# Instruction order from the timeline simulation in place of the default scheduler

## The chip, the cores and the metric

One core of one Trainium2 chip runs the whole program. The metric is device time in microseconds (us) of one execution, as the median of several runs. Matmuls run on TensorE (PE, its weight loads shown apart as PEld), elementwise work on VectorE (DVE) and ScalarE (ACT), a little on GpSimd (POOL), and SyncE (SP) issues nearly all DMAs.

## The reference, cut to what matters

Two layers of a hybrid trunk are computed for 128 context tokens and 256 latent tokens of width 1024. All weights are shared, so the kernel treats the tokens as one matrix of 384 columns; the two kinds differ in their modulation, in attention and in the sequence length of the convolutions.

```python
def trunk_layer(x, cond, l, P, cache):
    mod = (jax.nn.silu(cond) @ P['w_mod'][l] + P['b_mod'][l])[:, None, :]
    sh1, sc1, g1, sh2, sc2, g2, sh3, sc3, g3 = jnp.split(mod, N_MOD, axis=-1)
    h = rmsnorm(x, P['g_ffn1'][l]) * (1 + sc1) + sh1
    x = x + 0.5 * g1 * swiglu(h, P['w1_gate'][l], P['w1_up'][l], P['w1_down'][l])
    h = rmsnorm(x, P['g_mix'][l]) * (1 + sc2) + sh2
    m, kv = token_mix(h, l, P, cache)
    x = x + g2 * m
    h = rmsnorm(x, P['g_ffn2'][l]) * (1 + sc3) + sh3
    x = x + 0.5 * g3 * swiglu(h, P['w2_gate'][l], P['w2_up'][l], P['w2_down'][l])
    return x, kv
```

`token_mix` projects h to 2048 columns and splits them into attention (8 query heads, 2 key heads, window and cached context), a conformer convolution of 31 taps with layernorm, and a Hyena mixer (two gated long convolutions, done here by transforms). The three parts are joined by one output projection. The feed-forward width is 2816. Everything is float32.

## The kernel before, in words

Activations stay on chip feature-major: 8 tiles of 128 features by 384 tokens. Every large product is made of 128x128 weight blocks. Each float32 operand is split into a rounded high part and the low rest, and `mm3` (L262 to L265) issues three matmuls for one block: high by high, high by low, low by high. The weights come as one stream of 313 chunks of 8 blocks (512 KB each) in the order in which the program is traced. `blk` (L241) loads a chunk into one of 5 `raw` buffers, ScalarE rounds it to `hi` (L249), VectorE subtracts to get `lo` (L250); there are 4 `hi` and 4 `lo` buffers, so weights can stand ready up to four chunks ahead. One chunk feeds 24 matmuls.

The modulation vectors need 128 more loads of 512 KB (`mod_unit`, L317). They share the 5 `raw` buffers with the stream, and VectorE makes two multiply-accumulate passes (L324) over each. These units are spread over the feed-forward stages by a table (`MODS`).

The stages follow each other: a start (`startup`: modulation of the first sublayer, the Hyena filters, the first four column tiles of the first product, and dummy matmuls from `spin`, L1055), feed-forward 1 of layer 0, mix of layer 0, feed-forward 2, and the same for layer 1, ending with `last_down`. In a feed-forward stage the order of the matmuls is fixed by data: gate and up tile by tile into two PSUM buffers each (`acc`, `S`), then the down projection. In a mix stage, generators for Hyena (`hyena`, `spectral`: transposes L695, transforms L674, products on VectorE L706 to L712, inverse transforms L720), the conformer (L764, L362, L382), attention scores (L843, softmax on VectorE and ScalarE, transposes L900), values (L910) and the output projection are traced between the 16 tiles of the input projection, by the list `PROGRAM`.

What sets the order on the chip: each engine runs its own instructions strictly in the order in which the program lists them, and waits on semaphores for data and buffers of the others. That list isn't the traced order. The framework traces the kernel, gives each instruction a priority by its place in the trace (`high_priority` moves it ahead: 94 places for loading and splitting a chunk, 100 for loading a modulation unit, 400 for the second half of a pair), and then plays the program on a simulated core. Whenever an engine of that core can take work, it is handed the instruction of the best priority among those whose inputs and buffers are there. The order in which work was handed out becomes the order of the lists; buffers are given out in the same pass. So the order depends on how long the simulated core takes over each step. `keep_in_program_order` pins the dummy matmuls behind what was traced before them on TensorE, and `after` pins pairs of small matmuls together.

## Time and profile before

| what | value |
|---|---|
| time, median of 3 runs (lowest, highest) | 1510.45 us (1509.03, 1514.73) |
| the profiled execution: time, span of its instructions | 1510.81 us, 1509.0 us |
| TensorE busy, weight loads busy | 98%, 93% of the span |
| VectorE, ScalarE busy | 74%, 45% |
| mean granted TensorE clock | 0.993 |
| DMA moved | 260.97 MB, mean 173 GB/s |

The profile covers one execution. Busy time is the union of an engine's instruction spans; a matmul's span overlaps the next one's, so a busy TensorE may still run under its pace. The clock is the share of full speed that was granted.

### The profile page before, as it was taken

The numbers are of one execution on the slowest core, as the hardware profiler recorded it, in microseconds if no ns is written. First come the engines' busy times: TensorE is split into PE (matmuls) and PEld (weight loads), VectorE is DVE, ScalarE is ACT, GpSimd is POOL, SyncE is SP. The second block draws the span as 40 slices with busy tenths as digits, with TensorE's granted clock in tenths as the row PEclk, the third lists the DMA queues.
The fourth block names the chain that finished last, engine by engine and source line by source line (L and its number), as shares of the span: only waits on it lengthen the run. The fifth ranks groups of instructions, "written<-read, shape, count | busy, mean of one in ns | idle before, by whom it ended". The sixth has DMA issues, their size and how long they took to land.

```text
span 1509.0 us, 22131 instructions
## 1 busy us (share of the span) xinstructions
PE 1482.5 (98%) x8372; PEld 1401.0 (93%) x8372; DVE 1116.2 (74%) x2115; ACT 673.3 (45%) x1164; POOL 29.7 (2%) x72
## 2 busy tenths in 40 slices
PE   8999999999999999999999999999999999999997
PEld 4799999999968999999999999999996799999885
DVE  6799998776896789897558998755599577555342
ACT  6673333335476653224336333333547665333331
POOL 0100000000000000000000000000000000000000
PEclk9899999999999999999999999999999999999999
DMA  9847876565312357676444777644431135444531
GB/s 312 301 151 249 270 261 227 189 204 181 118 64 70 112 189 237 219 235 209 154 135 133 247 244 237 225 154 155 143 125 49 59 109 167 154 154 140 182 112 42
DMA packets 72651, 260.97 MB, mean 173 GB/s; under 512 B 8224, under 2 KB 9760, under 8 KB 72544
## 3 DMA queue, kind: packets, MB, share of 16 engines
q1 hardware_dynamic: 71360, 254.30, 51.4%
q0 software_dynamic: 1184, 5.25, 0.9%
q8 instruction: 66, 1.08, 0.3%
q14 instruction: 41, 0.34, 0.1%
HBM read 252.96 MB, written 6.56 MB: 172 GB/s over the span
## 4 chain that ended last, share of the span: by engine, by line
PE 92%; DVE 3%; ACT 3%; DMA 1%; issue 1%; SPq 0%; POOL 0%; POOLq 0%; DVEq 0%; ACTq 0%
PE acc L263 14%; PE acc L264 14%; PE acc L265 14%; PE S L265 12%; PE S L263 12%; PE S L264 12%; PE sp L474 2%; PE at L474 2%; PE sp L674 2%; PE acc L474 1%; PE S L474 1%; PE sp L720 1%; DVE lo L250 1%; DMA raw<-wmod 1%; DMA raw<-wms 0%
## 5 line engine op out<-in xcount | busy, mean ns | idle before, releaser
L250 DVE TENSOR_TENSOR lo<-raw,hi 128x1024 fp32r<-128x1024 f32 x313 | 381.7, 1222 | 209.1 <-ACT hi L249 160.2
L249 ACT CAST hi<-raw 128x1024 fp32r<-128x1024 f32 x313 | 327.0, 1049 | 390.7 <-issue 131.3
L324 DVE SCALAR_TENSOR_TENSOR junk<-raw,cb 128x1024 f32<-128x1024 f32 x256 | 312.7, 1221 | 49.8 <-DMA raw<-wmod 46.8
L263 PE MATMUL acc<-h,hi 128*128 128x384 f32 (+1 forms) x960 | 331.0, 345 | 0.0
L265 PE MATMUL acc<-h,lo 128*128 128x384 f32 (+1 forms) x960 | 326.0, 340 | 0.5 <-DVE lo L250 0.5
L264 PE MATMUL acc<-h,hi 128*128 128x384 f32 (+1 forms) x960 | 325.4, 340 | 0.6 <-DVE h L918 0.6
L263 PE MATMUL S<-h,hi 128*128 128x384 f32 (+1 forms) x768 | 259.9, 338 | 1.0 <-DVE x L435 1.0
L265 PE MATMUL S<-h,lo 128*128 128x384 f32 (+1 forms) x768 | 259.5, 338 | 0.0
L264 PE MATMUL S<-h,hi 128*128 128x384 f32 (+1 forms) x768 | 259.4, 338 | 0.0
L264 PEld LDWEIGHTS acc<-h,hi 128*128 128x128 f32 x960 | 181.0, 189 | 5.8 <-issue 3.1
L263 PEld LDWEIGHTS acc<-h,hi 128*128 128x128 f32 x960 | 180.5, 188 | 6.1 <-issue 3.9
L265 PEld LDWEIGHTS acc<-h,lo 128*128 128x128 f32 x960 | 181.5, 189 | 2.0 <-issue 0.8
L263 PEld LDWEIGHTS S<-h,hi 128*128 128x128 f32 x768 | 144.5, 188 | 2.0 <-issue 1.9
L265 PEld LDWEIGHTS S<-h,lo 128*128 128x128 f32 x768 | 145.0, 189 | 0.4 <-issue 0.3
L264 PEld LDWEIGHTS S<-h,hi 128*128 128x128 f32 x768 | 144.6, 188 | 0.4 <-issue 0.4
L393 ACT ACTIVATE h<-x,mod 128x128 fp32r<-128x128 f32 x96 | 41.5, 453 | 91.3 <-DVE x L435 89.4
L531 DVE TENSOR_TENSOR t<-S,t 128x384 f32<-128x384 f32 x72 | 39.8, 552 | 20.5 <-PE S L265 20.5
L281 ACT CAST P<-t 128x384 fp32r<-128x384 f32 x24 | 12.3, 514 | 71.4 <-DVE t L531 71.4
L530 ACT ACTIVATE t<-acc 128x384 f32<-128x384 f32 x72 | 34.8, 483 | 11.2 <-PE acc L265 11.2
L394 DVE SCALAR_TENSOR_TENSOR h<-x,mod,h 128x128 fp32r<-128x128 f32 x96 | 38.3, 415 | 1.2
L414 DVE TENSOR_TENSOR t<-acc,rb 128x384 f32<-128x384 f32 x44 | 24.3, 552 | 16.3 <-PE acc L265 16.3
L408 ACT ACTIVATE t<-t,mod,mod 128x128 f32<-128x128 f32 x64 | 31.7, 541 | 6.4 <-DVE t L405 6.4
(492 smaller groups left out, 2196.6 us busy)
## 6 DMA issues: line engine op xcount, KB each, us to landing
raw<-stream SPq DMA_DIRECT2D x313, 512.0 KB, 4.0
raw<-wmod SPq DMA_DIRECT2D x128, 512.0 KB, 4.3
raw<-wms SPq DMA_DIRECT2D x16, 512.0 KB, 6.6
Hd<-sw POOLq DMA_DIRECT2D x6, 768.0 KB, 4.6
H<-Hd SPq DMA_DIRECT2D x6, 768.0 KB, 4.9
x<-x SPq DMA_DIRECT2D x8, 192.0 KB, 6.2
y<-h SPq DMA_DIRECT2D x6, 256.0 KB, 2.1
cb<-crow SPq DMA_DIRECT2D x2, 512.0 KB, 5.3
```

Of the source, the lines that this page charges most:

```text
L249: nc.scalar.copy(out=hi, in_=raw)
L250: nc.vector.tensor_tensor(out=lo, in0=raw, in1=hi.bitcast(F32), op=ALU.subtract)
L263: nc.tensor.matmul(out, lhsT=w[0], rhs=x[0], start=start, stop=False)
L264: nc.tensor.matmul(out, lhsT=w[0], rhs=x[1], start=False, stop=False)
L265: nc.tensor.matmul(out, lhsT=w[1], rhs=x[0], start=False, stop=stop)
L324: nc.vector.scalar_tensor_tensor(out=self.junk, in0=raw, scalar=1.0, in1=self.cb[:, ci, :], op0=ALU.mult, op1=ALU.mult, accum_out=m[:, 2 * ...
L393: nc.scalar.mul(out=hl[:, 0, a:b], in_=self.x[k][:, a:b], mul=sc)
L394: nc.vector.scalar_tensor_tensor(out=hl[:, 1, a:b], in0=self.x[k][:, a:b], scalar=sc, in1=hl[:, 0, a:b].bitcast(F32), op0=ALU.mult, op1=AL ...
L408: nc.scalar.activation(out=t[:, a:b], in_=t[:, a:b], func=AF.Identity, scale=A[:, i:i + 1], bias=B[:, i:i + 1])
L474: nc.tensor.matmul(accs[b], lhsT=hid[2 * c + e][xi][:, b * 128:(b + 1) * 128], rhs=w[e][wi], start=c == 0 and left[b] == 5, stop=c == NFF ...
L530: nc.scalar.activation(out=s, in_=gp[:, :T], func=AF.Silu)
L531: nc.vector.tensor_tensor(out=s, in0=up[:, :T], in1=s, op=ALU.mult)
```

## The change

The context in which the kernel is traced gets one more argument. It selects the machine that the scheduler plays the program on: the framework's timeline simulation instead of the simulated core that it uses by default. The traced program, its priorities, its buffers, its pins and every instruction's work are the same; the handing out of work follows the other machine's times, and so the order of the instructions in each engine's list, the places of the DMA issues in SP's list, and which buffer each tile gets may be others.

```diff
--- before.py
+++ after.py
@@ -1197,7 +1197,7 @@
     outs = {"y": (3, 128, D), "nk": (DEPTH, 128, NP), "nv": (DEPTH, 128, NP)}
     for n, s in outs.items():
         d[n] = nc.dram_tensor(n, s, F32, kind="ExternalOutput").ap()
-    with tile.TileContext(nc) as tc, ExitStack() as ctx:
+    with tile.TileContext(nc, schedule_with_timeline_sim=True) as tc, ExitStack() as ctx:
         k = Kernel(ctx, tc, d)
         k.run()
     arrays["stream"] = pack_stream(k.plan, i)
```

## Rows read from the trace of the kernel before

**Rows 1.** The page's first part: engine, busy us, share of span, instructions.
```profile
PE 1482.5 (98%) x8372; PEld 1401.0 (93%) x8372; DVE 1116.2 (74%) x2115; ACT 673.3 (45%) x1164; POOL 29.7 (2%) x72
```
**Rows 2.** Busy time by stage, from the start to the last evacuation (header first).
```profile
core 0: us, PE busy (x) PEld busy (x) DVE busy (x) ACT busy (x) POOL busy (x), PEclk, DMA share, GB/s
0.00:73.00 73.00, 65.75 (x372) 43.17 (x373) 50.33 (x154) 46.88 (x83) 6.11 (x12) 0.91 0.87 306
73.00:346.00 273.00, 272.66 (x1549) 269.34 (x1547) 242.76 (x415) 110.14 (x166) 4.78 (x5) 1.00 0.68 223
346.00:507.00 161.00, 157.71 (x921) 140.25 (x922) 124.03 (x315) 95.01 (x214) 5.39 (x23) 1.00 0.32 104
507.00:780.00 273.00, 273.00 (x1562) 272.44 (x1561) 212.76 (x354) 109.37 (x163) 1.77 (x1) 1.00 0.60 193
780.00:1059.00 279.00, 279.00 (x1598) 278.47 (x1597) 217.41 (x363) 108.83 (x164) 1.45 (x2) 1.00 0.61 195
1059.00:1224.00 165.00, 159.30 (x926) 140.49 (x925) 124.30 (x312) 95.81 (x214) 4.33 (x23) 1.00 0.29 95
1224.00:1499.00 275.00, 275.00 (x1454) 256.88 (x1453) 140.35 (x202) 103.88 (x155) 3.65 (x4) 1.00 0.40 132
1499.00:1509.00 10.00, 0.09 (x1) 0.00 (x0) 4.23 (x8) 3.39 (x7) 2.19 (x3) 0.63 0.41 157
```
**Rows 3.** TensorE's waits, whole run: us in total, times, longest; first and last.
```profile
PE at L293 <- DMA raw<-wms: 2.3, 2, 1.7
PE acc L910 <- ACT pt L903: 2.1, 3, 1.3
...
PE at L900 <- ACT pt L903: 0.5, 2, 0.2
```
**Rows 4.** TensorE's timeline in layer 1's mix: start us, length us, what.
```profile
1130.97 0.42 PE L263 MATMUL acc<-h,hi 128*128 128x386 f32 x1
1131.23 0.34 PE L264 MATMUL acc<-h,hi 128*128 128x386 f32 x1
1131.41 1.94 PE L720 MATMUL sp<-csts,sw 128*128 128x128 f32 x16
1133.11 0.42 PE L265 MATMUL acc<-h,lo 128*128 128x386 f32 x1
1133.37 0.34 PE L263 MATMUL acc<-h,hi 128*128 128x386 f32 x1
```
**Rows 5.** Busy time in shorter stretches, columns as in rows 2.
```profile
60.00:70.00 10.00, 10.00 (x23) 5.09 (x19) 7.08 (x14) 5.14 (x9) 1.00 (x2) 0.56 0.71 252
150.00:200.00 50.00, 50.00 (x286) 50.00 (x285) 49.65 (x79) 17.94 (x24) 0.00 (x0) 1.00 0.83 272
600.00:650.00 50.00, 50.00 (x289) 50.00 (x287) 41.98 (x63) 16.75 (x24) 0.00 (x0) 1.00 0.69 220
1140.00:1150.00 10.00, 8.57 (x45) 5.27 (x45) 9.19 (x26) 6.17 (x21) 0.00 (x0) 1.00 0.14 52
1160.00:1170.00 10.00, 8.79 (x54) 5.39 (x53) 9.70 (x33) 8.63 (x23) 0.00 (x0) 1.00 0.16 54
```
**Rows 6.** Costliest groups on VectorE and ScalarE: busy us, mean ns, idle before.
```profile
L250 DVE TENSOR_TENSOR lo<-raw,hi 128x1024 fp32r<-128x1024 f32 x313 | 381.7, 1222 | 209.1 <-ACT hi L249 160.2
L249 ACT CAST hi<-raw 128x1024 fp32r<-128x1024 f32 x313 | 327.0, 1049 | 390.7 <-issue 131.3
L324 DVE SCALAR_TENSOR_TENSOR junk<-raw,cb 128x1024 f32<-128x1024 f32 x256 | 312.7, 1221 | 49.8 <-DMA raw<-wmod 46.8
```
**Rows 7.** The page's DMA issues: count, KB each, us from issue to landing.
```profile
raw<-stream SPq DMA_DIRECT2D x313, 512.0 KB, 4.0
raw<-wmod SPq DMA_DIRECT2D x128, 512.0 KB, 4.3
```

## The prediction

> **What bounds the kernel now.** I read the page's busy shares first, then the same busy times cut by stage, then TensorE's waits, and last the timeline of a mix stage. The shares say that TensorE is the bound: busy 1482.5 of 1509.0 us, VectorE behind it with 74% [rows 1]. The reader should see in the stages that this isn't one regime. The four feed-forward stages (273, 273, 279 and 275 us, together 1100 us) have TensorE busy throughout, but for 0.34 us in the first [rows 2]. There 289 matmuls start in 50 us, one per 0.173 us [rows 5]; a chunk of 24 lasts 4.2 us. The rest is the start (73 us, 7.3 us idle), the two mixes (161 us with 3.3 idle, 165 us with 5.7 idle) and a tail of 10 us in which TensorE has one matmul and VectorE, ScalarE and the output DMAs finish [rows 2]. TensorE's waits are short: fifteen rows between 2.3 and 0.5 us in total, the longest single one 1.7 us, for a DMA of the start; the second row is a chain of the mix, TensorE waiting for ScalarE's copy ahead of the values [rows 3]. So no stage but the start, the mixes and the tail can get shorter by order, and every stage can get longer.
>
> In the mixes the engine that decides is VectorE: 9.19 and 9.70 of 10 us busy in two stretches of layer 1's mix, where TensorE is down to 8.57 and 8.79 [rows 5]. The chains (Hyena, conformer, attention) go through VectorE at each step, and what is ahead of a chain's step in its list delays the chain.
>
> **The change part by part.** Nothing is removed or added: the same 8372 matmuls and the same 2115 VectorE instructions [rows 1] in another order. Its price is only what waits come or go, stage by stage. Not known from the trace is how the other machine spaces its steps. What the trace does show is how the order before treats a chain. In layer 1's mix the sixteen inverse-transform matmuls stand between the second and the third matmul of one block [rows 4]: the chain's step was put in front of filler at the first moment it was ready, and the filler, 0.173 us each, gave way. A machine that takes work into a queue ahead of a busy engine fixes the order earlier: filler that is ready gets in first, and the chain's step stands behind it although its priority is better. I take it that the timeline simulation does so to some degree. It is an assumption about the scheduler; the last rival drops it.
>
> Mixes. In a mix the Hyena chain passes between TensorE and VectorE at six steps (transposes, transforms, inverse transforms, twice). No row shows such a step standing behind filler. From below: a gain of all of the mixes' idle time, 3.3 + 5.7 = 9.0 us [rows 2]. From above: one whole chunk of filler, 4.2 us, at each of six steps in both mixes, 12 x 4.2 = 50 us. In between stands the longest piece of VectorE's filler, one `lo` of 1.222 us [rows 6]; with VectorE at 92 to 97% there [rows 5], an early chosen `lo` would lie in the way at each step. I take that, 12 x 1.222 = 14.7 us, because it is the nearest row in size to the waits that chains make now (longest 1.3 us, rows 3). The cover for the rest is TensorE's own filler, of which the projection's tiles provide 16; it is used up about when TensorE's waits begin, near 1140 us, and after that each delay of the chain shows in full.
>
> Start. In 60 to 70 us the granted clock was 0.56, a mean of its two levels (1.2 and 2.4 GHz), and 23 matmuls ran [rows 5]; at full clock the same stretch would have been (1 - 0.56) x 10 = 4.4 us shorter. Another order can spare this or make a second one: from -4.4 - 2.3 (the waits for the first DMAs, rows 3) = -6.7 to, say, two more, +8.8 us. The filters' and modulation's chains share VectorE as the mixes' do, so I take half of one more: +2.2 us.
>
> Here a rule bears on the mixes. The granted clock stays at 1.00 there in spite of TensorE's idle 1.2 to 1.4 us per 10 [rows 5], so lost time is priced at its own length. The Trainium skill (TensorE: Matmul & The Clock Gate, What's actually happening) says that half rate is the default state and activity releases it, so longer idling would also slow the matmuls that follow. By the row a wait costs itself; by the rule the new order's waits, were they much longer than these, would cost up to one stretch like that at 60 us per mix more, 2 x 4.4 us by that row, and the sum would be 1536 us. The start agrees with the rule, the mixes don't reach it, and I leave it out of the sum.
>
> Feed-forward. The weights stand up to four chunks ahead; with one in use that is 3 x 4.2 = 12.6 us of cover. A `lo` put behind one modulation unit is 2 x 1.221 us late [rows 6], and behind two units 4.9 us, which the cover hides, and so it hides a late load of 4.0 us [rows 7]. Below: there is 0.34 us to gain. I take 0. What it costs without the cover is the second rival. The tail: its chain is a fixed sequence for three blocks of 128 tokens, 0.
>
> Sum: 14.7 + 2.2 = 16.9 us, on the profiled execution's 1510.81 us (span 1509.0 and 1.8 around it) 1527.7; that execution lies 0.4 us above the median of the runs, which gives 1527 us. Own range: 1516 (a third of the sum) to 1557, where attention's twelve units per mix are each a `lo` late as well (24 x 1.222 = 29.3 us more).
>
> **The rivals.** *The loads bunch up and the feed-forward starves.* Stream and modulation share five raw buffers, and VectorE is busy 49.65 of 50 us at 150 to 200 us [rows 5], so lost cover isn't rebuilt at once. Were five modulation units loaded in a row, VectorE would owe 5 x 2.44 = 12.2 us before the next chunk's buffer is free; then come the load (4.0 us, rows 7), `hi` (1.05) and `lo` (1.22, rows 6): 18.5 us against a cover of 12.6, a stall of 5.9 us. The 128 units make at most 25 such bunches; a third of them, 8 x 5.9 = 47 us, gives 1557, and with the forecast's terms 1574. For it: the DMA issues are reordered too. Against it: the units are traced a few per tile, and the stream's loads have nearly the same lead in priority.
>
> *Faster: the chains are placed better.* If the timeline simulation's times are nearer to the chip's than the default's, the order has fewer steps that come to an engine before their input. It decides from the point where the chains' waits on TensorE shrink instead of grow. Price: all of the mixes' idle time, 9.0 us, and about half of the start's 7.3 us idle (its DMAs move 306 GB/s, rows 2, and set part of it), together 12.6 us: 1498. Against it: VectorE is nearly full in those stretches, and no order makes its work less. The weight loads show more room than the busy time: idle 161 - 140.25 and 165 - 140.49, together 45 us in the mixes [rows 2]. The Trainium skill (Perfetto Trace Analysis, Identifying the Most-Contended Engine) says to judge TensorE's headroom by the weight loads' share and not by matmul busy time; by that the limit here would be 45 us and the time down to 1465. The trace agrees only in part: by the matmul rows 9.0 of the 45 us are idle, and how much of the rest is gap no row tells.
>
> *No change.* The order comes out the same where it matters, or the moves lie under the covers named above: the priorities, pins and buffers are the same, and the feed-forward (73% of the span) is held by data. Then 1510 us, at most some 5 us to either side.
>
> **How the numbers follow.** Forecast 0.38, starved feed-forward 0.14, faster 0.26, no change 0.22. About 0.5% (7.6 us) is what a measurement of this kernel tells from no change, so faster is below 1502.9 and slower above 1518.0. The forecast gives 0.36 to slower and 0.02 to the same (its low end lies under 1518), the starved case 0.14 to slower, the faster case 0.22 to faster and 0.04 to the same, no change 0.22 to the same: 0.22, 0.28, 0.50. The range reaches from 1495, somewhat below the faster case, to 1576, the starved case with the forecast's terms.
>
> **What would show it.** Right: the feed-forward stages keep 273 to 279 us and 289 matmuls per 50 us; the mixes grow by about 7 us each; TensorE's timeline there shows chain steps only between whole runs of filler, no longer inside a block; the longest waits are on VectorE's and ScalarE's chain steps. A stretch of low clock in the start tells that term. A wait for `lo` in a feed-forward stage, behind L324 on VectorE, is the starved case. Mixes under 160 us with idle time near zero are the faster case, and identical lists the last. The prediction is wrong if the change in time comes from the feed-forward or the tail, or if the mixes get shorter.

## The result and the profile after

| | median us (lowest to highest, runs) |
|---|---|
| changed kernel | 1546.43 (1544.86 to 1548.21, 4) |
| kernel before, beside it | 1511.12 (1509.03 to 1514.73, 4) |

The ratio is 1.0231, with a 95% interval of 1.0215 to 1.0246: the new order costs 35 us. The forecast was 1527, +16.5 us on its own base, so the direction was right, and the forecast size was less than half of what came. The profiled execution took 1548.21 us (span 1546.3, mean granted clock 0.976); the one of before had 1510.81 (1509.0, 0.993).

First the page of the changed kernel: its first part, the group of the `lo` on VectorE, and the DMA issues of the stream.

```profile
PE 1494.9 (97%) x8372; PEld 1416.1 (92%) x8372; DVE 1111.1 (72%) x2115; ACT 684.7 (44%) x1168; POOL 28.3 (2%) x72
...
L250 DVE TENSOR_TENSOR lo<-raw,hi 128x1024 fp32r<-128x1024 f32 x313 | 382.2, 1223 | 194.0 <-ACT hi L249 147.9
...
raw<-stream SPq DMA_DIRECT2D x313, 512.0 KB, 4.2
```

The same 8372 matmuls and 2115 VectorE instructions as in [rows 1], with 1223 ns for a `lo` (1222 in [rows 6]) and 4.2 us for a landing (4.0 in [rows 7]): none of these operations got dearer. Two numbers of TensorE moved. TensorE's idle time (span less busy) went from 26.5 to 51.4 us, +24.9, and its busy time from 1482.5 to 1494.9, +12.4 for the same matmuls. Together that is the whole 37.3 us of span.

Next the changed kernel by stage (columns as in [rows 2], the cuts at its own stage ends), then shorter stretches of the start, of two feed-forwards and of the two mixes.

```profile
0.00:92.00 92.00, 73.73 (x378) 49.31 (x378) 54.26 (x160) 54.49 (x89) 6.02 (x12) 0.78 0.76 263
92.00:363.00 271.00, 271.00 (x1535) 269.43 (x1535) 238.19 (x409) 107.53 (x164) 4.11 (x5) 0.99 0.68 221
363.00:533.00 170.00, 158.18 (x915) 141.92 (x914) 122.25 (x307) 95.73 (x214) 4.51 (x23) 0.97 0.29 92
533.00:810.00 277.00, 275.68 (x1577) 275.10 (x1577) 212.86 (x361) 112.50 (x165) 0.85 (x1) 1.00 0.59 192
810.00:1089.00 279.00, 279.00 (x1597) 278.73 (x1596) 215.45 (x363) 111.06 (x164) 2.30 (x2) 1.00 0.61 195
1089.00:1257.00 168.00, 158.68 (x910) 141.08 (x909) 121.03 (x305) 94.97 (x211) 5.54 (x23) 0.96 0.28 94
1257.00:1536.00 279.00, 278.21 (x1471) 260.55 (x1469) 142.56 (x209) 104.99 (x160) 2.69 (x3) 1.00 0.41 131
1536.00:1546.00 10.00, 0.39 (x2) 0.00 (x0) 4.53 (x9) 3.39 (x7) 2.29 (x3) 0.66 0.41 157
...
10.00:20.00 10.00, 3.69 (x18) 0.78 (x17) 2.35 (x6) 7.41 (x10) 0.00 (x0) 0.50 1.03 398
20.00:30.00 10.00, 8.97 (x60) 5.19 (x62) 4.47 (x17) 5.77 (x11) 0.00 (x0) 0.65 0.99 331
30.00:40.00 10.00, 5.27 (x22) 2.05 (x19) 8.03 (x30) 8.98 (x14) 0.00 (x0) 0.69 1.01 328
...
150.00:200.00 50.00, 50.00 (x286) 49.24 (x286) 48.77 (x80) 18.64 (x27) 1.06 (x2) 1.00 0.83 278
650.00:700.00 50.00, 50.00 (x288) 50.00 (x287) 46.64 (x72) 18.05 (x24) 0.00 (x0) 1.00 0.75 246
...
433.10:443.10 10.00, 6.72 (x38) 5.50 (x36) 8.71 (x22) 5.65 (x15) 0.00 (x0) 1.00 0.26 75
443.10:453.10 10.00, 7.45 (x39) 5.47 (x39) 7.91 (x26) 5.23 (x20) 0.00 (x0) 0.66 0.33 112
...
1158.80:1168.80 10.00, 6.75 (x37) 5.40 (x35) 8.48 (x23) 6.07 (x18) 0.00 (x0) 0.91 0.26 88
1168.80:1178.80 10.00, 9.16 (x39) 6.05 (x40) 7.77 (x23) 6.98 (x24) 0.00 (x0) 0.57 0.22 79
```

For the sums below the stages are cut at two marks that exist in every run: the first instruction of line 414 (the first four column tiles of the first feed-forward are finished, which ends the start) and the last residual (line 435) of each stage.

| stage, us | before | after | difference | of it TensorE idle |
|---|---|---|---|---|
| start, to the first L414 | 70.3 | 91.3 | +21.0 | +11.0 |
| rest of layer 0's first feed-forward | 275.8 | 271.9 | -3.9 | -0.4 |
| layer 0: mix, second feed-forward | 160.9, 273.3 | 169.7, 277.6 | +13.0 | +9.9 |
| layer 1: first feed-forward | 278.4 | 278.4 | 0 | 0 |
| layer 1: mix, second feed-forward and tail | 165.6, 284.7 | 168.0, 289.5 | +7.2 | +4.4 |

The reader should see that the feed-forwards run as before (286 and 288 matmuls in 50 us, clock 1.00). Where a second feed-forward is longer, it has got matmuls from the mix: 1580 instead of 1564 in layer 0, and at 0.173 us these 16 are 2.8 of its 4.2 us. The two places that lost time are the start and the mixes, and in both the stretches of low clock stand beside or behind stretches in which TensorE is idle.

TensorE's waits of the changed kernel (us in total, times, longest) answer to [rows 3]:

```profile
PE S L843 <- ACT P L865: 9.7, 4, 3.0
PE sp L720 <- DVE ut L709: 4.3, 2, 2.2
PE sp L954 <- ACT t L938: 4.1, 1, 4.1
PE at L300 <- ACT t L297: 3.4, 2, 3.1
```

Before, no single wait was longer than 1.7 us. Now the three longest are all for ScalarE: in the start 4.1 us for the filter's first sine (L938) and 3.1 for the copy of a modulation (L297), in the mixes 3.0 for the exponentials of the attention (L865).

**The start.** ScalarE's timeline of the changed kernel, to its first modulation copy (start us, length us, what, idle before):

```profile
5.09 1.28 ACT L975 ACT_TABLE_LOAD   x1
12.50 0.63 ACT L975 ACTIVATE pt<-pt 128x512 f32<-128x512 f32 x1 [6.12 <-DMA pt<-ld]
...
13.79 0.61 ACT L975 ACTIVATE pt<-pt 128x512 f32<-128x512 f32 x1
14.42 1.28 ACT L938 ACT_TABLE_LOAD   x1
15.71 0.52 ACT L938 ACTIVATE t<-t 128x384 f32<-128x384 f32 x1
16.25 1.28 ACT L976 ACT_TABLE_LOAD   x1
17.55 3.17 ACT L976 ACTIVATE P<-pt,csts 128x512 f32<-128x512 f32 x5
20.62 0.35 ACT L297 COPY t<-at 128x256 f32<-128x256 f32 x1
```

and the same two instructions in the kernel before:

```profile
10.51 0.52 ACT L938 ACTIVATE t<-t 128x384 f32<-128x384 f32 x1 [5.46 <-DVE t L936]
...
13.82 0.37 ACT L297 COPY t<-at 128x256 f32<-128x256 f32 x1 [0.85 <-PE at L293]
```

The sine stands behind an exponential whose operand is still on its way from DRAM, and comes 5.2 us later; the copy stands behind five decay exponentials and comes 6.8 us later. SyncE's list changed as well. Sixteen loads bring the weights of the first modulation (`raw<-wms`, L239). In the kernel before the seventh and the eighth of them follow each other; in the changed one, loads that are wanted later stand ahead of the eighth (SP's list from the two traces, cut: place in the list, load, us of the issue and of the landing):

```
before                                 after
17 raw<-wms, the 7th   13.81 20.57     17    x<-x (L1088)         13.15 20.64
18 raw<-wms, the 8th   15.98 21.84     18    raw<-wms, the 7th    14.45 21.95
19 raw<-stream         16.41 23.06     19-24 x<-x (L1088), 6      15.72 25.00
20 raw<-wms, the 9th   21.64 25.24     25    q<-ld (L943)         20.66 25.66
21 raw<-wms, the 10th  22.07 28.70     26    ut<-ld (L943)        21.96 26.39
22 x<-x (L1088)        23.50 29.16     27-28 cb<-crow (L1050), 2  22.46 30.08
...                                    29    csts<-cst (L1047)    23.52 35.30
38 q<-ld (L943)        38.75 48.90     30-31 cv<-cw (L1016), 2    24.03 37.75
...                                    32    raw<-wms, the 8th    25.42 38.80
52 csts<-cst (L1047)   70.58 78.56
```

The loads of x, q, ut, cb, csts and cv on the right are 7 x 192 + 2 x 256 + 2 x 512 + 960 + 2 x 288 = 4416 KB, 4.5 MB, which at 398 GB/s (the stretch from 10 to 20 us) is an estimated 11.4 us of loading. In the trace 16.9 us pass between the landings of the seventh and the eighth modulation load (21.95 and 38.80), where before it was 1.3 (20.57 and 21.84). The sixteenth was issued at 35.6 us before and at 58.7 us after, and the first feed-forward's first columns can't end before the last modulation.

**A mix.** TensorE's timeline of the changed kernel in layer 0's mix, first a place early in it, then the first two waits for the exponentials:

```profile
424.90 0.34 PE L264 MATMUL acc<-h,hi 128*128 128x386 f32 x1
425.08 1.05 PE L720 MATMUL sp<-csts,sw 128*128 128x128 f32 x8
425.89 0.42 PE L265 MATMUL acc<-h,lo 128*128 128x386 f32 x1
...
437.78 0.49 PE L843 MATMUL S<-kv,q 64*128 64x128 f32 x4
438.20 1.13 PE L674 MATMUL sp<-ut,csts 128*128 128x256 f32 x4
442.37 0.49 PE L843 MATMUL S<-kv,q 64*128 64x128 f32 x4 [3.03 <-ACT P L865]
445.41 1.65 PE L843 MATMUL S<-kv,q 64*128 64x384 f32 x4 [2.55 <-ACT P L865]
```

and VectorE's in between, where the scores' maximum (L860) has to become the exponential's bias (L861):

```profile
438.83 0.48 DVE L860 TENSOR_REDUCE st<-S 128x1 f32<-128x128 f32 x2
439.22 0.68 DVE L708 TENSOR_TENSOR sw<-sw,H 128x512 f32<-128x512 f32 x1
439.82 1.22 DVE L250 TENSOR_TENSOR lo<-raw,hi 128x1024 fp32r<-128x1024 f32 x1
440.96 0.15 DVE L861 SCALAR_TENSOR_TENSOR st<-st,nsink 128x2 f32<-128x2 f32 x1
```

The reader should see two things. The chain's next step (L861) stands behind a Hyena product and one `lo` of 1.22 us on VectorE; and TensorE has nothing left to do meanwhile, because the filler of this stretch (L263 to L265) was used up before 437.8 us. Of the four waits for these exponentials in the two mixes the first is the only one with a `lo` in its way; in the other three Hyena's operations alone (L682, L706, L708, L710) stand there. In the kernel before, filler stands on TensorE's list between eight of the eleven neighbouring groups of score matmuls in this mix (in the changed kernel between four of ten), for instance here:

```profile
426.39 0.49 PE L843 MATMUL S<-kv,q 64*128 64x128 f32 x4
426.81 0.44 PE L265 MATMUL acc<-h,lo 128*128 128x386 f32 x1
...
429.43 0.92 PE L843 MATMUL S<-kv,q 64*128 64x384 f32 x4
```

### The profile page after: what moved, and what is told of

Same layout as the page of the kernel before. It is cut to its first block, busy times and chain, and to the rows that moved or that the text cites. A ratio compares the mean times of both kernels' runs of the same rounds, so it can differ in the third digit from the quotient of the medians.

```text
span 1546.3 us, 22180 instructions
## 1 busy us (share of the span) xinstructions
PE 1494.9 (97%) x8372; PEld 1416.1 (92%) x8372; DVE 1111.1 (72%) x2115; ACT 684.7 (44%) x1168; POOL 28.3 (2%) x72
## 4 chain that ended last, share of the span: by engine, by line
PE 91%; DVE 5%; ACT 2%; issue 1%; DMA 1%; SPq 0%; POOL 0%; POOLq 0%; ACTq 0%; DVEq 0%
PE acc L263 14%; PE acc L264 14%; PE acc L265 14%; PE S L263 12%; PE S L264 12%; PE S L265 12%; PE sp L474 2%; PE at L474 2%; PE sp L674 1%; PE sp L720 1%; PE acc L474 1%; PE S L474 1%; DVE P L854 1%; DMA pt<-ld 1%; PE S L843 0%
## 5 line engine op out<-in xcount | busy, mean ns | idle before, releaser
L250 DVE TENSOR_TENSOR lo<-raw,hi 128x1024 fp32r<-128x1024 f32 x313 | 382.2, 1223 | 194.0 <-ACT hi L249 147.9
L263 PE MATMUL acc<-h,hi 128*128 128x384 f32 (+1 forms) x960 | 330.8, 345 | 3.2 <-DVE small L420 2.1
L265 PE MATMUL acc<-h,lo 128*128 128x384 f32 (+1 forms) x960 | 326.1, 340 | 0.0
L263 PE MATMUL S<-h,hi 128*128 128x384 f32 (+1 forms) x768 | 260.5, 339 | 0.0
L265 PE MATMUL S<-h,lo 128*128 128x384 f32 (+1 forms) x768 | 259.7, 338 | 0.0
L263 PEld LDWEIGHTS acc<-h,hi 128*128 128x128 f32 x960 | 181.7, 189 | 10.5 <-issue 4.1
L265 PEld LDWEIGHTS acc<-h,lo 128*128 128x128 f32 x960 | 181.9, 190 | 1.2 <-issue 1.0
L263 PEld LDWEIGHTS S<-h,hi 128*128 128x128 f32 x768 | 145.0, 189 | 0.2
L265 PEld LDWEIGHTS S<-h,lo 128*128 128x128 f32 x768 | 145.0, 189 | 0.0
L531 DVE TENSOR_TENSOR t<-S,t 128x384 f32<-128x384 f32 x72 | 39.9, 554 | 21.1 <-PE S L265 21.0
L414 DVE TENSOR_TENSOR t<-acc,rb 128x384 f32<-128x384 f32 x44 | 24.3, 553 | 17.3 <-PE acc L265 13.5
L843 PE MATMUL S<-kv,q 64*128 64x384 f32 (+1 forms) x96 | 21.0, 516 | 10.5 <-ACT P L865 9.7
```

The lines of the kernel that those rows point to most:

```text
L250: nc.vector.tensor_tensor(out=lo, in0=raw, in1=hi.bitcast(F32), op=ALU.subtract)
L263: nc.tensor.matmul(out, lhsT=w[0], rhs=x[0], start=start, stop=False)
L265: nc.tensor.matmul(out, lhsT=w[1], rhs=x[0], start=False, stop=stop)
L531: nc.vector.tensor_tensor(out=s, in0=up[:, :T], in1=s, op=ALU.mult)
```

## The experiments

All but the ninth and tenth are built in one way. The kernel is traced once with the one scheduler, only to read the order in which it hands out the instructions; then it is traced again with the other, and for chosen engines and a chosen part of the trace each instruction is tied behind the one that the first order has ahead of it. Work, buffers and data stay; the engines that aren't chosen follow the second scheduler.

```diff
+def pin(tc, insts, donor, engine):
+    mine = {i.name: i for i in insts}
+    last = None
+    for name, eng, kind in donor:
+        if eng != engine or name not in mine or "Release" in kind or "Boundary" in kind:
+            continue
+        if last is not None:
+            tc.add_manual_dep(mine[name], last, mybir.DependencyInfo(
+                mybir.DependencyClass.NoSync, mybir.DependencyReason.DATA), reason="order")
+        last = name
```

`PINS` says which: engine, from and to which traced instruction, whose order. Instructions 12 to 2640 are layer 0's first feed-forward with the whole start-up and both layers' filters; 2640 to 3956 and 8232 to 9545 are the mixes. `BASE_TIMELINE` says which scheduler does the rest. The lists of pins are written here in a shorter form, and `MIXES` is short for those two ranges. Each run was compared with the kernel before on the same chip.

| run | us | ratio to before (95%) | start, to the first L414 | mix of layer 0, 1 | last modulation load issued |
|---|---|---|---|---|---|
| e1_start | 1527.79 | 1.0116 (1.0101 to 1.0131) | 70.2 | 169.2, 166.5 | 36.1 |
| e2_mixes | 1535.06 | 1.0158 (1.0137 to 1.0180) | 90.2 | 161.4, 170.1 | |
| e3_start_sp | 1544.72 | 1.0224 (1.0208 to 1.0240) | 82.8 | 169.7, 167.7 | 40.1 |
| e4_start_act | 1540.21 | 1.0202 (1.0184 to 1.0219) | 81.6 | 169.0, 166.5 | 46.4 |
| e5_start_both | 1532.78 | 1.0143 (1.0128 to 1.0158) | 71.7 | 170.8, 168.2 | 34.6 |
| e6_start_and_mixes | 1513.77 | 1.0016 (1.0004 to 1.0028) | 67.2 | 162.6, 168.5 | |
| e7_mix_pe | 1561.98 | 1.0334 (1.0307 to 1.0362) | 89.8 | 177.1, 178.9 | |
| e8_before_new_mix_pe | 1548.05 | 1.0243 (1.0226 to 1.0260) | 68.2 | 183.9, 183.6 | |
| e9_before_filler_early | 1520.17 | 1.0061 (1.0046 to 1.0077) | 67.4 | 169.6, 168.9 | |
| e10_before_filler_spread | 1518.62 | 1.0062 (1.0038 to 1.0086) | 67.3 | 167.5, 167.5 | |
| e11_before_new_loads | 1521.74 | 1.0076 (1.0050 to 1.0102) | 77.0 | 161.0, 165.6 | 48.3 |
| e12_start_four_lines | 1545.30 | 1.0229 (1.0214 to 1.0244) | 85.0 | 172.5, 167.1 | |
| e13_start_clock | 1543.34 | 1.0219 (1.0202 to 1.0236) | 86.8 | 170.4, 167.7 | |
| e14_mix_dve_act | 1553.80 | 1.0287 (1.0271 to 1.0302) | 89.0 | 171.7, 179.0 | |
| e15_before_new_dve_act | 1540.18 | 1.0191 (1.0176 to 1.0206) | 68.6 | 175.2, 176.0 | |

The stage columns are of the one profiled execution. (In the expectations of e3, e4 and e11 the load that waits is called the tenth modulation load; it is the eighth.)

### Where: the start or the mixes

e1_start:
```diff
 BASE_TIMELINE = True
+PINS = [(e, 12, 2640, "default") for e in ("PE", "DVE", "Activation", "SP", "Pool")]
```


> Changed kernel, but the instructions of layer 0's first feed-forward (start-up, filters of both layers and what it streams) stand on every engine in the order of the kernel before; mixes and the rest keep the new order. Theory (losses add up by place): the start's 17 us come back, so 1546 - 17 = about 1529 (1526 to 1532), and the first column of the feed-forward ends at about 70 us instead of 91. Rival (the start is only where the delay shows; the filter work that was done early in it is owed later): the mixes get longer by what the start gets shorter, so 1540 or more.

e2_mixes:
```diff
+PINS = [(e, *r, "default") for r in ((2640, 3956), (8232, 9545)) for e in ("PE", "DVE", "Activation", "SP", "Pool")]
```


> Changed kernel, but the instructions of both mixes stand in the order of the kernel before on every engine; start and feed-forwards keep the new order. Theory: the 13 + 7 us of mixes and what follows them come back, 1546 - 20 = about 1526 (1523 to 1530); granted clock 1.00 at 440 to 460 us of this run's first mix. Rival (the first mix is long because the late start leaves its loads and filters late): under half of that comes back, 1537 or more.

e6_start_and_mixes has both lists of pins.

> Changed kernel with layer 0's first feed-forward and both mixes in the order of the kernel before on every engine; only the other three feed-forwards keep the new order. Theory (the feed-forwards cost nothing, losses add up): 1511, 1507 to 1516. Rival (the new order of the second feed-forwards' first columns and of what is read ahead costs 4 to 5 us in each of two): 1518 to 1522.

e1 took back 18.6 us, with the start at 70.2 us: the theory's number. e2 took back 11.4 of the 20 that were expected, between the two expectations: the first mix is back at 161.4 us with a clock of 1.00, the second is not. Its lists there are nearly those of the kernel before, and yet it is 4.5 us longer. These are the two kernels in the same twenty microseconds of that mix, first e2_mixes, then the kernel before:

```profile
1156.40:1166.40 10.00, 8.80 (x49) 5.75 (x47) 9.79 (x26) 5.39 (x19) 0.00 (x0) 0.98 0.16 52
1166.40:1176.40 10.00, 8.92 (x29) 5.61 (x27) 6.31 (x21) 6.54 (x19) 0.00 (x0) 0.50 0.00 1
```
```profile
1138.70:1148.70 10.00, 8.80 (x49) 5.76 (x48) 9.80 (x26) 5.44 (x19) 0.00 (x0) 1.00 0.14 52
1148.70:1158.70 10.00, 8.78 (x46) 5.61 (x44) 8.79 (x30) 8.47 (x24) 0.89 (x1) 1.00 0.00 0
```

The first ten are nearly alike in all columns; in the next ten the one gets the lower level of the clock and starts 29 matmuls, the other the higher and starts 46. So the mixes stand at an edge where the clock falls in one execution and not in another: e2's four runs reach from 1530.41 to 1536.66, with a mean clock of 0.986 in the shortest and 0.979 in the longest. With start and mixes turned back, e6 is 0.2% from the kernel before: the order of the other feed-forwards costs next to nothing, and the two losses add up (18.6 + 11.4 = 30.0 of the 32.7 that e6 took back). e6, with every list tied in three places, also shows that the tying by itself costs little.

### The start: which list

e3_start_sp, e4_start_act and e5_start_both, on the changed kernel:
```diff
+PINS = [("SP", 12, 2640, "default")]                                          # e3
+PINS = [("Activation", 12, 2640, "default")]                                  # e4
+PINS = [("Activation", 12, 2640, "default"), ("SP", 12, 2640, "default")]     # e5
```


> Changed kernel, but in layer 0's first feed-forward the loads on SyncE's queue alone stand in the order of the kernel before; ScalarE's first twenty instructions keep the new order (decay exponentials ahead of the first sine and of the first modulation's copy). Loads theory: the 4.5 MB (seven of x, both decays, two rows for cb, the late constants, both taps) that stand ahead of the tenth modulation load cost 4.5 MB / 398 GB/s = 11 us, so about 1535. ScalarE theory: the wait behind the exponentials costs most of it, so 1543 or more.

> Changed kernel, but in layer 0's first feed-forward ScalarE alone follows the order of the kernel before (first sine at once, first modulation's copy right behind the first exponential); SyncE's queue keeps the new order with 4.5 MB of late loads ahead of the tenth modulation load. ScalarE theory: the copy comes 6.8 us earlier and with it the slots that the next modulation loads wait for; 7 to 17 us come back, 1529 to 1539. Loads theory: 3 us or less come back, 1543 or more, and the tenth modulation load still lands after 40 us.

> Changed kernel, in layer 0's first feed-forward ScalarE and SyncE's queue both in the order of the kernel before, TensorE, VectorE and the rest of the kernel left to the new order. With one of the two lists alone (e3_start_sp 1544.7, e4_start_act 1540.2) the first column tile ended at 83 and 82 us instead of 91 (70 in the kernel before). Theory (two causes side by side, each hides behind the other): with both the first column tile ends by 72 us and the time is that of e1_start, 1528 (1526 to 1532). Rival (VectorE's and TensorE's new lists hold the start up as well): the column tile ends after 77 us and the time stays over 1534.

e11_before_new_loads is the mirror image on the kernel before:
```diff
 BASE_TIMELINE = False
+PINS = [("SP", 12, 2640, "timeline")]
```


> Kernel before (default scheduler), with SyncE's queue of layer 0's first feed-forward in the order of the changed kernel: 4.5 MB of late loads ahead of the tenth modulation load; ScalarE keeps the first sine and the first copy where they were. Loads theory: first column tile at 80 to 82 us instead of 70, in all 1517 to 1522. Rival (without ScalarE's delay the slots come free early and the loads land in time): first column tile by 74 us, 1514 or less.

The start ends at 91.3 us with both new lists, at 82.8 with SyncE's turned back, at 81.6 with ScalarE's, at 71.7 with both. By its time e3 met ScalarE's expectation, and e4 lay between the two; by the start neither theory is right alone: with one new list left the start is still 11 to 13 us over the 70.3 of the kernel before, and the two hide behind each other. The modulation loads show it, as first and last issue of the sixteen (the two numbers ahead of the semicolon), for e4 and e5:

```profile
L239 SPq DMA_DIRECT2D raw<-wms x16: 327/328/1124, 3.1 to 46.4; - x16
```
```profile
L239 SPq DMA_DIRECT2D raw<-wms x16: 327/350/465, 3.1 to 34.6; - x16
```

In time the single mends brought less than their starts: 1.7 us for SyncE's and 6.2 for ScalarE's, because the rest of the first feed-forward took 278.0 and 275.5 us instead of 271.9; with both lists it was 13.7 us, between the two expectations of e5 in time and on the theory's side in the start. Of the 5.8 us of span that e5 has over e1, 2.4 lie in the first feed-forward, where TensorE's and VectorE's new lists are left, and 3.3 in the mixes. e11 took the time that the loads theory said, 11.8 us more, with ScalarE's first sine and copy where they were. Its profiled execution was the shortest of four that reach from 1517.53 to 1527.11: its start is 77.0 us, not the 80 expected, and these 6.7 us more are all that its span has over the kernel before.

e12_start_four_lines turns four lines of ScalarE, in the start-up only:
```diff
+PINS = [("Activation", 12, 502, "default", 938, 975, 976, 297)]
```


> Changed kernel; on ScalarE alone, and of its start only the instructions of four lines (sines, the two kinds of decay exponentials, the copies of the modulations) stand in the order of the kernel before. Theory (the first sine behind exponentials that wait for their loads, and the first copy behind five of them, are the whole of ScalarE's part): as e4_start_act, 1540 (1537 to 1543). Rival (the rest of ScalarE's list in the first feed-forward counts too): 1544 or more.

The rival: 1545.3 us, a start of 85.0 us. The sine and the copy are a part of the start alone (6.2 us of the 9.7 that e4 got there), and in time nothing came back: e12 is 35.3 us over the kernel before on its chip, as the changed kernel is. So the rest of ScalarE's list in the feed-forward counts too.

e13_start_clock leaves all lists of the changed kernel and puts matmuls of no use into five of TensorE's waits:
```diff
+FILL = {("L293", 0): 5, ("L954", 0): 8, ("L300", 0): 6, ("L979", 4): 5, ("L674", 0): 3}
+PINS = [(e, 12, 2640, "timeline") for e in ("PE", "DVE", "Activation", "SP", "Pool")]
...
+                    self.fills.append(self.nc.tensor.matmul(accs[2][:, 388:512], lhsT=self.ones, rhs=self.ones[:, 0:124],
+                                                            start=True, stop=True, skip_group_check=True))
```


> Changed kernel, every list as it is, with 27 matmuls of no use (128 x 124, into unused columns of an accumulator) put on TensorE's list ahead of five of the matmuls that wait longest in the first 40 us: 27 x 0.42 = 11.4 us of work laid into 14.2 us of waits. Clock theory (the low clock that follows the waits carries a good part of the start's loss): granted clock over 0.9 between 10 and 40 us instead of 0.50 to 0.69, first column tile ends at 86 us or sooner instead of 91, in all 1541 or less. Wait theory (the chain of loads and ScalarE sets the start, TensorE only follows): clock up all the same, first column tile at 89 us or later, 1544 or more.

The same stretches as in the changed kernel above, of e13_start_clock:
```profile
10.00:20.00 10.00, 6.42 (x39) 5.02 (x39) 2.93 (x7) 8.47 (x13) 0.00 (x0) 0.83 1.02 395
20.00:30.00 10.00, 9.49 (x81) 5.61 (x82) 5.98 (x23) 8.12 (x14) 0.00 (x0) 1.00 1.03 380
30.00:40.00 10.00, 6.51 (x29) 3.57 (x28) 9.12 (x30) 7.67 (x11) 0.00 (x0) 0.83 0.94 308
```
The clock went from 0.50, 0.65, 0.69 to 0.83, 1.00, 0.83, and the start from 91.3 to 86.8 us; the time fell by 3.1 us, between the two expectations. The mean clock of the whole start came back from 0.78 to 0.90, where the kernel before has 0.91. So of the 21 us some 4.5 are the clock's, the larger part is the waiting for loads and for ScalarE.

### The mixes: one list or the order as a whole

e7_mix_pe and e14_mix_dve_act on the changed kernel, e8_before_new_mix_pe and e15_before_new_dve_act on the kernel before:
```diff
+PINS = [("PE", 2640, 3956, "default"), ("PE", 8232, 9545, "default")]                 # e7
+PINS = [(e, *r, "default") for e in ("DVE", "Activation") for r in MIXES]             # e14
+PINS = [("PE", 2640, 3956, "timeline"), ("PE", 8232, 9545, "timeline")]               # e8
+PINS = [(e, *r, "timeline") for e in ("DVE", "Activation") for r in MIXES]            # e15
```


> Changed kernel with TensorE's list alone in the order of the kernel before in both mixes; the other engines are left to the new scheduler, which follows. Theory (filler used up ahead of the chain's last steps, so TensorE stands and waits for ScalarE's exponentials, with the clock at half after it): as e2_mixes, 1535 or less, first mix 161 to 164 us instead of 170. Rival (the lists of VectorE and ScalarE delay the chains): first mix 167 us or more, 1542 or more.

> The mirror image: kernel before, with TensorE's list in the two mixes taken from the new order and everything else left to the default scheduler. Theory (TensorE's list is the cause in the mixes): first mix 168 us or more with waits of over 2 us on ScalarE's exponentials and a stretch of clock under 0.8, in all 1511 + 12 to 20 = 1523 to 1531. Rival: under 1517.

> Changed kernel with VectorE's and ScalarE's lists of both mixes in the order of the kernel before; TensorE's list is left to the timeline scheduler, which places it around them. With TensorE's list alone turned back (e7_mix_pe) the time rose to 1562. Theory (no single list is at fault, the three are one order and a crossing of two orders makes waits): 1546 or more. Rival (the chains' order on VectorE and ScalarE is what costs, TensorE's list only had to follow): 1537 or less.

> Mirror image: kernel before with VectorE's and ScalarE's lists of both mixes taken from the changed kernel; TensorE's list is left to the default scheduler. With TensorE's list alone taken over (e8_before_new_mix_pe) the time rose to 1548. Theory (crossing of two orders): more than the 20 us that the whole new order costs in the mixes, 1531 or more. Rival (the lists of VectorE and ScalarE cost nothing by themselves): under 1520.

e7's theory failed. Its rival's bounds held (first mix 177.1 us, 1562 us), but neither expected that with TensorE's old list the changed kernel becomes 15.6 us slower still. e8 is 37 us slower than the kernel before, over the 12 to 20 of its theory, where e1, with the whole new order of the mixes, is 16.4 us slower. e8's waits in the first mix, the first three:
```profile
PE S L843 <- ACT P L865: 4.3, 2, 2.9
PE at L900 <- ACT P L881: 3.7, 1, 3.7
PE S L843 <- DVE st L854: 3.0, 2, 2.1
```
From that came the theory that e14 and e15 tried: no single list is at fault. It held: VectorE's and ScalarE's old lists make the changed kernel 7.4 us slower, their new lists the kernel before 29 us. Each order is one whole over three engines, and where two of them cross, TensorE waits longer than in either: in the two mixes together it is idle for 8.9 us before, 21.1 in the changed kernel and 24.4 to 34.8 in the four crossings.

e9 and e10 leave the default scheduler and move traced steps, so that all lists follow:
```diff
-PROGRAM = ("v1 x10 a1 H g1 H H q1 k q0 C v A C q3 q2 C A A H A H C A A x21 A V A A x20 C V A H C V C A V A W W W "
+PROGRAM = ("v1 x10 a1 H g1 H H q1 k q0 x21 x20 C v A C q3 q2 C A A H A H C A A A V A A C V A H C V C A V A W W W "   # e9
+PROGRAM = ("v1 x10 a1 H g1 H H q1 k q0 C A C q2 C A A H q3 A H C A A x21 v A V x20 A A C V A H C V C A V A W W W "   # e10
```


> Kernel before (default scheduler), with the two last projection columns x21 and x20 traced right behind q0, so that 94 matmuls of the chains stand on TensorE's list in a row without a filler matmul (48 in the kernel before, 88 in the changed one). Theory (it is the using up of filler ahead of the chains that costs, by waits on the exponentials and a stretch of low clock behind them): first mix 168 us or more instead of 161, granted clock under 0.8 in a stretch of 10 us, in all 1511 + 12 to 20 = 1523 to 1531. Rival (it is in what order each engine takes the chains, which is little changed here): under 1516.

> Kernel before (default scheduler), with five of the traced steps v, q2, q3, x21 and x20 moved so that filler stands later and in more places: the longest stretch of chain matmuls without filler is 32 instead of 48. Filler theory: a third of the 8.9 us in which TensorE is idle in the two mixes goes, 1508 (1505 to 1511). Rival (at 48 the chains are covered well enough, another wait takes its place): 1511 to 1518.

e9 came out 10.2 us slower, under the 12 to 20 of the theory and over the rival's bound, with clocks of 0.83 instead of under 0.8 and the first mix at 169.6 us: using up filler early does cost, but it is not the whole of the mixes' loss. By length its mixes grew as much as the changed kernel's (8.7 and 3.3 us against 8.8 and 2.4); but TensorE is idle for 13.1 us in them, not 21.1, and the feed-forwards behind them keep their length. As all lists follow the moved steps, it isn't shown that the filler alone does it. e10 failed: with the longest stretch without filler cut from 48 to 32 matmuls it is 8.6 us slower, not faster. Where the filler stands counts, but the length of the longest gap doesn't say how. No version here beats the kernel before.

## Why the prediction was right or wrong

**The failed step is the start's term.** It stands at +2.2 us, "half of one more" stretch of low clock, with bounds from -6.7 to +8.8. The start grew by 21.0 us (17.1 at the end of the first feed-forward, where some filter work had been done ahead), and e1 shows 18.6 us of time in it: over twice the upper bound, and with 18.6 - 2.2 = 16.4 us most of the 18.8 by which the forecast fell short (35.3 against 16.5). The step priced a longer start only by TensorE's clock and looked for the cause on VectorE. It didn't go through what may come ahead of what on the two lists that feed the start, ScalarE's and SyncE's, where a step that waits for a DMA holds up all behind it. e3, e4, e5 and e11 show these two lists. The clock, which the step took for the price, was some 4.5 us of it (e13).

**The mixes' term** was 14.7 us of waits. In the mixes and the feed-forwards behind them TensorE's idle time grew by 9.9 + 4.4 = 14.3 us. The mechanism, a chain's step behind one `lo` on VectorE, is in the rows (L860, L708, L250, L861), but on attention's chain, with TensorE waiting for its exponentials, and in one of its four waits; the six Hyena steps that the term counted wait twice at the inverse transforms (L720, 4.3 us) and twice at the transforms (L674, 1.1 us). So the size is near by luck, and the count behind it was not what came: by time e1 shows 16.4 us outside the start. Wrong is the sign that was announced: the changed kernel still has chain steps inside a block of filler (425.08 us). And e7 with e14 says that the waits can't be put down to one engine's list.

**What was left out** is the clock in the mixes. The trace of before had 1.00 there; the changed one has 0.66 and 0.57 in ten microseconds beside waits of 3.0 and 2.5 us in layer 0 and of 1.9 and 2.2 us in layer 1, and the two mixes with their second feed-forwards have 13.0 + 7.2 - 14.3 = 5.9 us of longer busy time. The prediction named this cost and left it out of the sum; it belonged in it. The Trainium skill (TensorE: Matmul & The Clock Gate, What's actually happening) says that the low rate is the default and activity releases it; the mixes here and e13 agree, and the 2 x 4.4 us that the prediction worked out beside that rule compare with the 5.9.

**Right** were the feed-forward at 0, no wait for `lo` in it, the tail at 10 us with two matmuls, and that the mixes' longest waits are on chain steps of ScalarE and VectorE; the mixes themselves grew by 8.8 and 2.4 us, not by about 7 each. "The loads bunch up" did come, in the start and not where that rival put it: there 4.5 MB of other loads stood ahead. Whether the five buffers held loads up as well no run separates: SP's waits for L293, which frees a buffer, were 23.2 us in the changed start and 13.6 before. The faster case and the unchanged one are excluded.

**Open** is why the timeline simulation put these steps in this order: no run shows which of its assumed times is off the chip's. In the mixes it is also open which pairs of steps matter; that the order matters as a whole is shown, and no more. ScalarE's new list of the start was never put into the kernel before alone, as SyncE's was in e11.

## What to carry to other kernels

Before pricing a new order of instructions, go through the first 100 us list by list, the load queue and the engine with the short steps first: an instruction that waits for a load holds everything behind it, and late loads ahead of early ones hold these up by their bytes over the rate or more (here 4.5 MB, 11 us by the rate and 16.9 by the landings). An order that was made for several engines at once can't be mended on one of them: half of it cost 7 to 21 us more than all of it. And longer waits on TensorE are to be priced with the clock: here pairs of waits of 1.9 to 3.0 us came with ten microseconds at a clock of 0.57 to 0.66.

## What the runs showed of the hardware that was not expected

- The clock can fall where TensorE is 88% busy and its longest wait is 1.1 us: the second mix of e2_mixes had the level of 0.50 for ten microseconds after a stretch that the kernel before passed at 1.00 with the same busy times. That mix is 4.5 us longer than the 165.6 of the kernel before, with no more idle time of TensorE in it (5.4 us against 5.7); in e6 it is 2.9 us longer, at a mean clock of 0.98.
- ScalarE's list of the changed kernel has four more table loads, 1168 instructions instead of 1164, all in the first feed-forward: 4 x 1.28 = 5.1 us. The Trainium skill (ScalarE: Activation LUTs, What ACT_TABLE_LOAD costs) gives about 1283 ns for one and a drain of about 1380 ns beside it; the load agrees to the nanosecond, and of a drain the rows show nothing: the load of 14.42 us ends at 15.70 and its sine starts at 15.71, and the load starts within 0.02 us of the exponential's end.
